# Fewer gate columns before the mixers, modulation steps beside the gate columns, and a tanh in place of a sigmoid, in a two-layer hybrid backbone

## The chip, the cores and the metric

The kernel runs on one core of a Trainium2 chip. The metric is the device time of one execution in microseconds (us). Three runs of the kernel before took 2787.75, 2791.62 and 2795.09 us; their median, 2791.62 us, is the time before.

## The reference, cut to what matters

Two layers work on 512 latent tokens and 256 context tokens of width 1024, in fp32. The second layer gives up the context after its mixers.

```python
mod_l = c_act @ ada_w + ada_b                 # six vectors of 1024: shift, scale and gate, twice
h = modulate(rms_norm(x, norm1_g), sh1, sc1)
daq, dak, dav, lx, ly, gqkv, gz, gb, ga, gate = split_proj(h @ w_in)
da  = differential attention of daq, dak, dav
lru = gelu(ly) * (bidirectional RG-LRU of conv(lx))
gdn = (bidirectional gated DeltaNet of gqkv) * silu(gz)
merged = sum(sigmoid(gate[i]) * ((da, lru, gdn)[i] @ w_branch[i]) for i in range(3))
x = x + g1 * (merged @ w_out)
x = x + g2 * mlp(modulate(rms_norm(x, norm2_g), sh2, sc2))

def rglru_coeffs(xc, gate_w, gate_b, lam):
    r, i = sigmoid(block_diag(xc, gate_w) + gate_b)          # two gates
    log_a = -8.0 * r * softplus(-lam)
    return exp(log_a), sqrt(-expm1(2.0 * log_a)) * (i * xc)

def step(s, xs):                              # DeltaNet, one chunk of tokens, one direction
    v_new = u_n - w_n @ s
    o_n = qd_n @ s + at_n @ v_new
    return s * ge_n + kd_n.T @ v_new, o_n
```

## The kernel before, in words

**Matmuls.** An activation lies in SBUF as 128 channels by up to 768 tokens. Each fp32 product is made of three fp32r products: both factors are split into a high and a low part (`split`, L174 in the profile, a cast on ScalarE and a subtraction on VectorE) and high-high, high-low and low-high are summed in PSUM (`mm_feat`, L201; `mm_tok`, L218). One column block of 128 outputs is 24 pairs of matmuls in the first layer (512 and 256 tokens each) and 24 matmuls of 512 tokens in the second, where context is not needed.

**Weights.** `wunit` loads 512 KB into a tile `raw` of a pool of three (`rp`), splits it into `wh` and `wl` (pools of three), and is done with `raw`.

**Modulation steps.** `ada_steps` is a generator. One round is eight steps and gives a third of the 6144 modulation columns of a layer. A step loads two `raw` tiles of `ada_w` (512 KB each) and adds four 32x512 matmuls into one accumulator `pada` (L344), which is one tile of the PSUM pool `pq` of three (`sm(...)`). The tile is kept from the first step of a round to its eighth, whose result is transposed (`padt`) and added to `L.mod`. The first layer needs round 1 and round 2 of this generator. Round 1 is taken by the projections `gq` and `gv`; round 2 stands in `merge_last`, one step at each of its eight columns. The second layer's own generator is empty; its modulation is computed in the first layer's MLP.

**DeltaNet.** `gdn_inproj` projects q, k and v. `gdn_core` first makes the chunk matrices (transposes L571, products L579 and L582, then a triangular solve of 31 dependent steps on VectorE, L690 and L692, which ends in the transposes L697 and L699). Then comes the recurrence: 24 chunks, both directions side by side. One step is matmuls from the state (L796), copies on ScalarE (L804, L809), the outputs of the step before (L758, L766), matmuls that make the new state (L816, L827 on VectorE), and the start of the next step (L788, L744, L746). Its accumulators `pgd` are `bank`: all three tiles of the pool `pq`, and the one tile of the pool `pf`.

**What is put between.** Behind `gdn_core` in the program stand column blocks that don't need it: `NG[l]` gate columns (`fill_gate`, names `pgt`, `gty`, stored to `gts`), the RG-LRU inputs and gates (`plx`, `py`, `plg`, `lsg`, stored to `lrs`), `gz`, k, v and q. Then come the parts that need the recurrence or the stored columns (`gdn_out`, `lru`, `da_load`, `da_keys`, whose transposes are `pdt`), and the remaining gate columns up to 24. `da_attend` with `merge_first`, `merge_last` (`pml`), the output projection (`pop`) and the MLP (`pm`) follow.

**What sets the order.** The program is traced once, and a scheduler orders the instructions of each engine. It takes what stands first in the program and is ready in its own timing model. A tile of a pool is given out when one is free; an instruction whose tile isn't free yet can't be placed, and others are taken before it. On the chip each engine runs its instructions in the order so fixed.

Of the kernel before, what the change touches and what calls it, by code (L numbers as in the profile page):

```python
# [12 lines left out]
AF = mybir.ActivationFunctionType  # L13
OP = mybir.AluOpType
# [3 lines left out]
T = 768  # L18
# [1 line left out]
TL = 512  # L20
D = 1024
EPS = 1e-6
NG = (12, 16)
NCH = 24
CTXCH = 8
HEADS = 4
# [22 lines left out]
def hybrid_prefix_dit_block_kernel(  # L49
# [8 lines left out]
    V, S, G, PE = nc.vector, nc.scalar, nc.gpsimd, nc.tensor  # L58
# [22 lines left out]
    def big(name):  # L81
        return pb.tile([P, 1024], F32, name=name, tag="b")
# [42 lines left out]
    for q in range(4):  # L125
        r = slice(32 * q, 32 * q + 16)
# [98 lines left out]
    def in_tile(l, col, early=True):  # L225
        return [wunit(w_in[l, :, col:col + P], early)]
# [41 lines left out]
    def load_cols(L, l, rows, mark=None, mark_v=None):  # L268

        r0, r1 = (r[:, :P] for r in rows)  # L270
        ps = big("pcol")
        i = PE.transpose(ps[:, 0:P], r0, ident)
        if mark is not None:
            behind(i, mark)
        PE.transpose(ps[:, P:2 * P], r1, ident)
        L.cols = lp.tile([P, 256], F32, name="cols", tag="cols")
        i = V.tensor_copy(L.cols, ps[:, 0:256])
        if mark_v is not None:
            behind(i, mark_v)
        L.n1 = L.cols[:, 0:8]  # L280
        L.n2 = L.cols[:, 8:16]
        L.adab = L.cols[:, 16:64]
        L.gb = L.cols[:, 80:96]
        L.lam = L.cols[:, 96:104]
        L.gng = L.cols[:, 104:105]
        L.subg = L.cols[:, 105:106]
        L.lcw = L.cols[:, 128:144]
        L.lcb = L.cols[:, 144:148]
        L.gcw = L.cols[:, 148:196]
        V.tensor_scalar(L.gcw, L.gcw, 0.5, None, op0=OP.mult)  # L290
        V.tensor_scalar(L.gng, L.gng, 0.5, None, op0=OP.mult)
        L.mod = lp.tile([P, 48, 2], F32, name="mod", tag=f"mod{l}")
        return L
# [567 lines left out]
        return Z  # L861


    def fill_gate(l, L, a, full, n):
        t0, nt = (0, T) if full else (TC, TL)
        us = in_tile(l, OFF["gate"] + P * n)
        ps = big("pgt")
        mm_feat(ps, us, 0, a, pieces(t0, nt))
        y = t3("gty")
        with tc.high_priority():  # L870
            S.activation(y[:, 0:nt], ps[:, 0:nt], AF.Tanh, scale=0.5)  # L871
        nc.sync.dma_start(gts[n][:, t0:T], y[:, 0:nt])
# [32 lines left out]
    def fill_lx_gates(l, L, j, y, weights):  # L905
        wh, wl = weights
        yh, yl = (gp.tile([P, T], F32R, name="gy", tag="g") for _ in range(2))
        parts = ((0, TC, 512, y[:, 0:TC]), (TC, T, 0, y[:, 259:771]))
        for a0, a1, o, src in parts:
            S.copy(yh[:, a0:a1], src)  # L910
            G.tensor_tensor(yl[:, a0:a1], src, yh[:, a0:a1].bitcast(F32), op=OP.subtract)
        for d in range(2):
            for g in range(2):
                ps = big("plg")
                i = 2 * d + g
                for n, (w, x) in enumerate(((wh, yh), (wh, yl), (wl, yh))):
                    for a0, a1, o, src in parts:
                        PE.matmul(ps[:, o:o + a1 - a0], lhsT=w[:, i, :], rhs=x[:, a0:a1], start=(n == 0), stop=(n == 2))
                r = t3("lsg")
                for a0, a1, o, src in parts:  # L920
                    with tc.high_priority():
                        S.activation(r[:, a0:a1], ps[:, o:o + a1 - a0], AF.Sigmoid,
                                     bias=L.gb[:, 8 * d + 4 * g + j:8 * d + 4 * g + j + 1])
                    if g == 1:
                        G.tensor_tensor(r[:, a0:a1], r[:, a0:a1], src, op=OP.mult)
                nc.sync.dma_start(lrs[j][:, 2 * d + g, :], r[:, 0:T])

    def fill_ly(l, L, a, full, j):
# [57 lines left out]
    def lru_tables(L):  # L986
        L.s8 = lp.tile([P, 8], F32, name="s8", tag="s8")
        L.ns8 = lp.tile([P, 8], F32, name="ns8", tag="ns8")
        nl = tiny("nlam", 8)
        V.tensor_scalar(nl, L.lam, -1.0, None, op0=OP.mult)  # L990
        softplus(L.s8, nl, 8, t3("spl")[:, 0:256])
        V.tensor_scalar(L.ns8, L.s8, 8.0, None, op0=OP.mult)
        V.tensor_scalar(L.s8, L.s8, -8.0, None, op0=OP.mult)

    def lru(l, L, full, mark):
        last = [None]
        t0 = 0 if full else TC
        lh = slab("lh").rearrange("p (k t) -> p k t", k=4)

        def act(*args, **kw):  # L1000
            i = S.activation(*args, **kw)
            if last[0] is not None:
                behind(i, last[0])
            last[0] = i

        for j in range(4):
            W = []
            for d in range(2):
                W.append(slab("lW").rearrange("p (k t) -> p k t", k=4))
                after(nc.sync.dma_start(W[d][:, 0:2, :], lrs[j][:, 2 * d:2 * d + 2, :]), mark)  # L1010
            r, ix, at, u = ([W[d][:, i, :] for d in range(2)] for i in range(4))
            for d in range(2):
                c = slice(4 * d + j, 4 * d + j + 1)
                act(at[d], r[d], AF.Exp, scale=L.s8[:, c])
                act(r[d], r[d], AF.Tanh, scale=L.ns8[:, c])
                act(u[d], at[d], AF.Square)
                V.scalar_tensor_tensor(r[d], u[d], 1.0, r[d], op0=OP.add, op1=OP.mult)
            for d in range(2):
                act(r[d], r[d], AF.Sqrt)
                (V if d else G).tensor_tensor(r[d], r[d], ix[d], op=OP.mult)  # L1020
            yl = ix[1]
            nc.sync.dma_start(yl[:, t0:T], lys[j][:, t0:T])
            hs, a1, b1, u1 = lh[:, j, :], at[1], r[1], u[1]
            V.tensor_tensor_scan(hs, at[0], r[0], 0.0, op0=OP.mult, op1=OP.add)
            V.tensor_tensor_scan(u1[:, TC - 1::-1], a1[:, TC - 1::-1], b1[:, TC - 1::-1], 0.0, op0=OP.mult, op1=OP.add)
            V.tensor_tensor_scan(u1[:, T - 1:TC - 1:-1], a1[:, T - 1:TC - 1:-1], b1[:, T - 1:TC - 1:-1], u1[:, 0:1],
                                 op0=OP.mult, op1=OP.add)
            G.tensor_tensor(hs[:, t0:T], hs[:, t0:T], u1[:, t0:T], op=OP.add)
            V.scalar_tensor_tensor(hs[:, t0:T], yl[:, t0:T], 0.5, hs[:, t0:T], op0=OP.mult, op1=OP.mult)
        return lh  # L1030

    def operands(parts, full):
# [202 lines left out]
                    G.tensor_tensor(gv[0], gv[0], gv[1], op=OP.add)  # L1235
                nc.sync.dma_start(mss[n][:, t0:T], g[0][:, t0:T])

    def merge_last(l, od, full, side):
        t0, nt = (0, T) if full else (TC, TL)
        M = Act("mg", 8)  # L1240
        for b in range(4):
            us = [wunit(w_branch[l, 0, :, 256 * b:256 * b + 256])]
            for n in (2 * b, 2 * b + 1):
                side()
                g, m = gate_of(0, n, t0), t3("ml")
                nc.sync.dma_start(m[:, t0:T], mss[n][:, t0:T])
                ps = big("pml")
                mm_feat(ps, us, P * (n % 2), od, pieces(t0, nt))
                V.scalar_tensor_tensor(g[:, t0:T], g[:, t0:T], 1.0, ps[:, 0:nt], op0=OP.add, op1=OP.mult)
                V.tensor_tensor(m[:, t0:T], m[:, t0:T], g[:, t0:T], op=OP.add)  # L1250
                split(M.hi(n)[:, t0:T], M.lo(n)[:, t0:T], m[:, t0:T])
        return M

# [74 lines left out]
    for i in range(2):  # L1328
        xr.append(slab("xr").rearrange("p (a d) -> p a d", a=3))
        for k in range(3):  # L1330
            t = 3 * i + k
            src = ctx[0, t * P:(t + 1) * P, :] if t < 2 else x[0, (t - 2) * P:(t - 1) * P, :]
# [5 lines left out]
    for half in range(2):  # L1338
        raws.append([])
        for k in range(8):  # L1340
# [3 lines left out]
            src = ada_w[0, k * P:(k + 1) * P, 0:2048].rearrange("p (q c) -> p q c", q=2)  # L1344
# [10 lines left out]
    for t in range(6):  # L1355
        xt = xr[t // 3][:, t % 3, :]
        s = slice(t * P, (t + 1) * P)
        for hf in range(2):
            jk = t3("xsq")
            S.activation(jk[:, 0:512], xt[:, 512 * hf:512 * hf + 512], AF.Square, accum_out=x2[:, 6 * hf + t:6 * hf + t + 1])  # L1360
            ps = sm("pxt")
            for i in range(4):
                n = 4 * hf + i
# [14 lines left out]
    L = Lay()  # L1378
    spill = [(xs[k // 4][:, k % 4, :], x0[k // 4][:, k % 4, :]) for k in range(8)]
    for l in range(DEPTH):  # L1380
        full = l < DEPTH - 1
        a = norm(xT, L, L.n1, 0, 8, "hn", halves(True)) if l else norm0(xT, L, raws, {0: mark_pe, 2: marks[-1]}, lambda i: load_cols(L, 0, vrows, i, mark_v))
        dump(f"hn{l}", a.h[0].bitcast(F32))
        steps = ada_steps(l, L, (1, 2) if l == 0 else ())
# [5 lines left out]
        gdn_core(l, L, R, full)  # L1390
        dump(f"go{l}", R.o)
        for n in range(NG[l]):
            fill_gate(l, L, a, full, n)
        Q = da_tables(l)
        lru_tables(L)
        y = fill_lx(l, L, a, full, 0)
# [30 lines left out]
        od = da_finish(L, Q, full)  # L1427
        dump(f"odh{l}", od.h[0].bitcast(F32))
        if stop == "da":
            return  # L1430
        M = merge_last(l, od, full, lambda: next(steps, None))
        xT = out_proj(l, L, M, full)
        dump(f"xa{l}_0", xT[0])
        dump(f"xa{l}_1", xT[1])
# [2 lines left out]
        a = norm(xT, L, L.n2, 24, 32, "hm", halves(full))  # L1437
# [5 lines left out]
        steps = ada_steps(l + 1, L2, (0, 1, 2)) if full else iter(())  # L1443
# [7 lines left out]
        if full:  # L1451
            L = L2
            spill = [(xs[k // 4][:, k % 4, :], xT[k // 4][:, k % 4, :]) for k in range(8)]

    for t in range(2, 6):
        for hf in range(2):
            ps = sm("pfo")
            for i in range(4):
                PE.transpose(ps[:, i * P:(i + 1) * P], xT[hf][:, i, t * P:(t + 1) * P], ident)
            o = t3("fo")  # L1460
# [28 lines left out]
```

## Time and profile before

| | before |
|---|---|
| time, median of three runs | 2791.62 us |
| time of the profiled execution | 2792.77 us |
| span of its trace | 2791.1 us |
| PE busy | 2651.8 us (95%) |
| DVE busy | 1487.5 us (53%) |
| ACT busy | 1104.9 us (40%) |
| POOL busy | 553.6 us (20%) |

PE is TensorE's matmuls, PEld its weight loads, DVE is VectorE, ACT is ScalarE, POOL is GpSimd. Times in the trace count from the start of the span. A busy PE is not a PE at its peak: matmuls are pipelined and their spans overlap. PEclk is the granted TensorE clock as a share of full speed.

### The profile page before, as it was taken

To read this page: it belongs to the slowest core of one execution; us is meant where nothing else is said; L and a number is where in the kernel's file an instruction comes from. 1 tells how busy PE (TensorE), PEld (TensorE's weight loads), DVE (VectorE), ACT (ScalarE), POOL (GpSimd) and SP (SyncE) were. 2 spreads that over 40 slices of the span, in tenths; PEclk is the share of its full clock that TensorE was granted. 3 is DMA by queue.
4 is the path that set the end of the run, shared out by engine and by line. 5 is a ranking of instruction groups with operands and counts; after the bars stand their busy time and mean duration, and the time that the engine had idled before them with its cause. 6 is when DMAs were issued, how large, how long until landed. Compare 5 with 4: busy or idle time off the path is not lost. (4 is left out here: it accounts for less than half of the span.)

```text
span 2791.1 us, 44891 instructions
## 1 busy us (share of the span) xinstructions
PE 2651.8 (95%) x17973; PEld 2256.7 (81%) x17973; DVE 1487.5 (53%) x2477; ACT 1104.9 (40%) x2058; POOL 553.6 (20%) x693
## 2 busy tenths in 40 slices
PE   7999999997999899999999999999998798899999
PEld 4778888996888688888888888777997687788887
DVE  5659554567375443333333476775437776544444
ACT  4343454465465233221122253445436755432321
POOL 3001343223112022110101130034322311221110
PEclk8999999998999999999999999999999699999999
DMA  7432233254423723333332222334224443333332
GB/s 261 127 111 89 84 104 101 77 168 142 145 99 106 250 81 110 125 106 114 121 114 76 89 78 76 107 104 144 84 68 145 166 125 103 98 106 92 97 99 76
DMA packets 315592, 318.71 MB, mean 114 GB/s; under 512 B 19500, under 2 KB 268408, under 8 KB 314488
## 3 DMA queue, kind: packets, MB, share of 16 engines
q1 hardware_dynamic: 315384, 315.84, 36.0%
q8 instruction: 142, 2.33, 0.4%
q14 instruction: 66, 0.54, 0.1%
HBM read 259.70 MB, written 56.10 MB: 113 GB/s over the span
## 5 line engine op out<-in xcount | busy, mean ns | idle before, releaser
L174 ACT CAST wh<-raw 128x1024 fp32r<-128x1024 f32 x288 | 302.6, 1051 | 969.0 <-PE pm L201 624.3
L174 DVE TENSOR_TENSOR wl<-raw,wh 128x1024 fp32r<-128x1024 f32 x288 | 368.0, 1278 | 453.6 <-ACT wh L174 441.2
L201 PE MATMUL pm<-hdh,wh 128*128 128x256 f32 (+1 forms) x896 | 297.4, 332 | 0.5
L201 PE MATMUL pm<-hdl,wh 128*128 128x256 f32 (+1 forms) x896 | 294.5, 329 | 0.0
L201 PE MATMUL pm<-hdh,wl 128*128 128x256 f32 (+1 forms) x896 | 294.3, 328 | 0.0
L1315 DVE SCALAR_TENSOR_TENSOR xT<-pm,mod,xT 128x256 f32<-128x256 f32 (+1 forms) x224 | 133.8, 598 | 237.5 <-PE pm L201 237.5
L201 PE MATMUL pm<-hmh,wh 128*128 128x512 f32 (+1 forms) x800 | 242.5, 353 | 4.4 <-ACT mr L1297 2.8
L201 PE MATMUL pm<-hml,wh 128*128 128x512 f32 (+1 forms) x800 | 243.6, 354 | 3.1 <-DVE hml L457 3.1
L1299 POOL TENSOR_TENSOR mq<-mr 128x768 f32<-128x768 f32 (+1 forms) x64 | 107.2, 1675 | 692.4 <-ACT mr L1297 684.7
L201 PE MATMUL pm<-hmh,wl 128*128 128x512 f32 (+1 forms) x800 | 240.7, 350 | 0.0
L201 PEld LDWEIGHTS pm<-hdh,wh 128*128 128x128 f32 x896 | 170.1, 190 | 30.2 <-DVE xT L1315 7.5
L201 PE MATMUL pgt<-hnh,wh 128*128 128x512 f32 x576 | 181.1, 365 | 8.8 <-ACT gty L871 8.8
L201 PEld LDWEIGHTS pm<-hdh,wl 128*128 128x128 f32 x896 | 170.0, 190 | 15.2
L201 PEld LDWEIGHTS pm<-hdl,wh 128*128 128x128 f32 x896 | 170.2, 190 | 14.8
L201 PE MATMUL pgt<-hnl,wh 128*128 128x512 f32 x576 | 178.8, 364 | 0.0
L201 PE MATMUL pgt<-hnh,wl 128*128 128x512 f32 x576 | 178.4, 363 | 0.0
L201 PEld LDWEIGHTS pm<-hmh,wh 128*128 128x128 f32 x800 | 134.9, 191 | 32.2 <-ACT wh L174 5.9
L201 PEld LDWEIGHTS pm<-hml,wh 128*128 128x128 f32 x800 | 135.5, 191 | 23.4 <-DVE hml L457 4.1
L201 PEld LDWEIGHTS pm<-hmh,wl 128*128 128x128 f32 x800 | 136.4, 191 | 21.5
L201 PEld LDWEIGHTS pgt<-hnh,wh 128*128 128x128 f32 x576 | 98.5, 193 | 26.9 <-ACT gty L871 10.3
L201 PE MATMUL pg<-hnh,wh 128*128 128x256 f32 (+1 forms) x368 | 103.9, 348 | 8.9 <-ACT hnh L407 4.7
L201 PEld LDWEIGHTS pgt<-hnh,wl 128*128 128x128 f32 x576 | 97.7, 193 | 16.3
(428 smaller groups left out, 6103.1 us busy)
## 6 DMA issues: line engine op xcount, KB each, us to landing
raw<-in_mlp_w_dram SPq DMA_DIRECT2D x128, 512.0 KB, 3.8
raw<-in_w_in_dram SPq DMA_DIRECT2D x120, 512.0 KB, 4.0
raw<-in_ada_w_dram SPq DMA_DIRECT2D x80, 512.0 KB, 3.9
lrs<-lsg SPq DMA_DIRECT2D x32, 384.0 KB, 2.4
lW<-lrs SPq DMA_DIRECT2D x16, 768.0 KB
raw<-in_w_branch_dram SPq DMA_DIRECT2D x24, 512.0 KB, 5.4
gts<-gty SPq DMA_DIRECT2D x24, 384.0 KB, 4.8
mgg<-gts SPq DMA_DIRECT2D x24, 384.0 KB, 3.5
```

The costliest lines, as they stand in the source:

```text
L174: return S.copy(hi, src), V.tensor_tensor(lo, src, hi.bitcast(F32), op=OP.subtract)
L201: last = PE.matmul(ps[:, o:o + n], lhsT=w, rhs=r[:, t0:t0 + n], start=(k == 0 and i == 0), stop=(k == nk - 1 and i == 2))
L1299: G.tensor_tensor(q[:, 0:nt], r[:, 0:nt], r[:, 0:nt], op=OP.mult)
L1315: V.scalar_tensor_tensor(xv, ps[:, 0:m], L.mod[:, 40 + n, v:v + 1], xv, op0=OP.mult, op1=OP.add)
```

## The change

There are four edits.

1. `NG` goes from (12, 16) to (10, 12): that many gate columns stand before the RG-LRU inputs; the other 14 and 12 stand behind the mixers.
2. The step of round 2 is taken out of `merge_last` and put into `fill_gate`, behind the weight unit of the column. The first eight gate columns of the first layer take the eight steps.
3. The RG-LRU gates are `tanh(0.5 x)` in place of `sigmoid(x)`; the factors 0.5 and the added 1 move into the bias, the decay factors (8 becomes 4, with a bias) and the last factor (0.5 becomes 0.25).
4. The product of the input gate with its input, 32 instructions in all, goes from GpSimd to VectorE, which adds 1 in the same instruction.

```diff
-NG = (12, 16)
+NG = (10, 12)
...
+        V.tensor_scalar(L.gb, L.gb, 0.5, None, op0=OP.mult)
...
-    def fill_gate(l, L, a, full, n):
+    def fill_gate(l, L, a, full, n, side=None):
         t0, nt = (0, T) if full else (TC, TL)
         us = in_tile(l, OFF["gate"] + P * n)
+        if side:
+            side()
         ps = big("pgt")
...
-                        S.activation(r[:, a0:a1], ps[:, o:o + a1 - a0], AF.Sigmoid,
+                        S.activation(r[:, a0:a1], ps[:, o:o + a1 - a0], AF.Tanh, scale=0.5,
                                      bias=L.gb[:, 8 * d + 4 * g + j:8 * d + 4 * g + j + 1])
                     if g == 1:
-                        G.tensor_tensor(r[:, a0:a1], r[:, a0:a1], src, op=OP.mult)
+                        V.scalar_tensor_tensor(r[:, a0:a1], r[:, a0:a1], 1.0, src, op0=OP.add, op1=OP.mult)
...
-        V.tensor_scalar(L.ns8, L.s8, 8.0, None, op0=OP.mult)
-        V.tensor_scalar(L.s8, L.s8, -8.0, None, op0=OP.mult)
+        V.tensor_scalar(L.ns8, L.s8, 4.0, None, op0=OP.mult)
+        V.tensor_scalar(L.s8, L.s8, -4.0, None, op0=OP.mult)
...
-                act(at[d], r[d], AF.Exp, scale=L.s8[:, c])
-                act(r[d], r[d], AF.Tanh, scale=L.ns8[:, c])
+                act(at[d], r[d], AF.Exp, scale=L.s8[:, c], bias=L.s8[:, c])
+                act(r[d], r[d], AF.Tanh, scale=L.ns8[:, c], bias=L.ns8[:, c])
...
-            V.scalar_tensor_tensor(hs[:, t0:T], yl[:, t0:T], 0.5, hs[:, t0:T], op0=OP.mult, op1=OP.mult)
+            V.scalar_tensor_tensor(hs[:, t0:T], yl[:, t0:T], 0.25, hs[:, t0:T], op0=OP.mult, op1=OP.mult)
...
-    def merge_last(l, od, full, side):
+    def merge_last(l, od, full):
...
-                side()
                 g, m = gate_of(0, n, t0), t3("ml")
...
-            fill_gate(l, L, a, full, n)
+            fill_gate(l, L, a, full, n, lambda: next(steps, None))
...
-        M = merge_last(l, od, full, lambda: next(steps, None))
+        M = merge_last(l, od, full)
```

The order that comes of it is shown at three places. In the change line numbers are 1 to 3 higher.

PE, first layer, from the last product of the chunk matrices on (`psq`); `pgt` is a gate column. Before:

```order
L597 MATMUL psq<-ones,gq_1810 32x1 x16
L201 MATMUL pgt<-hnh,wh 128x512
L201 MATMUL pgt<-hnh,wh 128x256
L201 MATMUL pgt<-hnl,wh 128x512
L201 MATMUL pgt<-hnl,wh 128x256
L201 MATMUL pgt<-hnh,wl 128x512
L201 MATMUL pgt<-hnh,wl 128x256
```

The same place in the change:

```order
L598 MATMUL psq<-ones,gq_1811 32x1 x16
L660 MATMUL pge<-ident,eg 128x128 x2
L789 MATMUL pgd<-gW 128x128 x2
L817 MATMUL pgd<-gW,gA 128x128 x3
L817 MATMUL pgd_2005<-gW,gA 128x128
L817 MATMUL pgd<-gW,gB 128x128 x3
L817 MATMUL pgd_2005<-gW,gB 128x128
L745 MATMUL pgd<-gW 128x128 x2
```

In the order before, 366 matmuls of gate columns stand between `psq` and the first matmul of the recurrence (`pgd`); in the change there are only the two of `pge`.

PE, first layer, within one step of the recurrence. Before:

```order
L796 MATMUL pgd<-gB,gW 32x128 x4
L796 MATMUL pgd<-gB,gQT 32x128 x4
L796 MATMUL pgd<-gA,gW 32x128 x4
L796 MATMUL pgd<-gA,gQT 32x128 x4
L758 MATMUL pgd_2004<-gW 128x128 x2
L201 MATMUL pgt<-hnh,wl 128x512
L201 MATMUL pgt<-hnh,wl 128x256
L201 MATMUL pgt<-hnh,wh 128x512
```

The last step of the recurrence in the change, and what follows it (`pada` is the accumulator of round 2):

```order
L797 MATMUL pgd<-gA,gQT 32x128 x4
L759 MATMUL pgd_2005<-gW 128x128 x2
L345 MATMUL pada<-raw,cact 32x512 x4
L759 MATMUL pgd_2005<-gW 128x128 x2
L345 MATMUL pada<-raw,cact 32x512 x4
L201 MATMUL pgt<-hnh,wh 128x512
L201 MATMUL pgt<-hnh,wh 128x256
```

Before, from `psq` to the last L758, 576 pairs of matmuls of 512 and 256 columns (gate columns, `plx`, `py`, `plg`, `pz`) and 635 matmuls of 256 columns (`pqk`, `pv`) stand among the matmuls of the recurrence. In the change none does in the first layer: the first `pada` is placed when the recurrence is over, and the gate columns from the third on behind it; no engine has a piece of them between its instructions of the recurrence.

SP, which issues the loads, first layer, around the second gate column. Before:

```order
L872 DMA gts_138<-gty 128x768
L166 DMA raw<-in_w_in_dram 128x8x128
L872 DMA gts_139<-gty 128x768
L166 DMA raw<-in_w_in_dram 128x8x128
L872 DMA gts_140<-gty 128x768
```

The same place in the change:

```order
L342 DMA raw<-in_ada_w_dram 128x1024
L166 DMA raw<-in_w_in_dram 128x8x128
L342 DMA raw<-in_ada_w_dram 128x1024 x2
L166 DMA raw<-in_w_in_dram 128x8x128
L342 DMA raw<-in_ada_w_dram 128x1024 x2
```

The loads of `ada_w` stand between those of the gate columns, in the same pool of three. In the second layer the recurrence stays interleaved with column blocks. Before, its last five groups of L796 stand without other matmuls between them, in the change its last seven; four gate columns of 24 matmuls have moved behind it.

## Rows read from the trace of the kernel before

**Rows 1.** The page's line of busy times.

```profile
PE 2651.8 (95%) x17973; PEld 2256.7 (81%) x17973; DVE 1487.5 (53%) x2477; ACT 1104.9 (40%) x2058; POOL 553.6 (20%) x693
```

**Rows 2.** Busy time by stretch; columns stand in the first row.

```profile
core 0: us, PE busy (x) PEld busy (x) DVE busy (x) ACT busy (x) POOL busy (x), PEclk, DMA share, GB/s
205.00:588.00 383.00, 378.03 (x3213) 328.06 (x3208) 218.65 (x486) 158.51 (x382) 112.08 (x190) 0.99 0.29 93
588.00:770.00 182.00, 163.63 (x1025) 147.50 (x1023) 113.13 (x149) 104.73 (x143) 51.00 (x26) 0.93 0.49 159
896.00:958.00 62.00, 53.24 (x293) 37.98 (x293) 30.31 (x40) 13.66 (x18) 4.27 (x5) 0.94 0.65 214
2127.00:2230.00 103.00, 82.02 (x363) 68.44 (x362) 82.63 (x106) 83.03 (x107) 37.13 (x22) 0.79 0.60 209
```

**Rows 3.** Busy time by stretch of the recurrence's accumulators alone: PE, PEld, DVE, ACT.

```profile
272.00:585.00 313.00, 100.33 (x1384) 78.77 (x1384) 61.69 (x230) 32.95 (x140) 1.00 0.30 95
```

**Rows 4.** Timeline of PE in a gate column: start, duration, line, operation.

```profile
212.30 0.52 PE L201 MATMUL pgt<-hnh,wh 128*128 128x512 f32 x2
213.37 0.51 PE L201 MATMUL pgt<-hnh,wh 128*128 128x512 f32 x2
```

**Rows 5.** Timeline of PE in a block of q.

```profile
2069.75 0.28 PE L218 MATMUL pqk<-wh,hnh 128*128 128x256 f32 x1
2070.47 0.28 PE L218 MATMUL pqk<-wh,hnh 128*128 128x256 f32 x1
```

**Rows 6.** Busy time of VectorE and ScalarE in line L174 during the solve.

```profile
205.00:272.00 67.00, 7.33 (x6) 7.37 (x7) 0.96 0.28 90
```

**Rows 7.** Timeline of PE, second layer, last five groups of L796.

```profile
2095.18 0.42 PE L796 MATMUL pgd<-gB,gW 128*32 128x128 f32 x8
...
2100.74 0.66 PE L796 MATMUL pgd<-gB,gW 128*32 128x128 f32 x8 [0.65 <-ACT gW L746]
...
2108.69 0.65 PE L796 MATMUL pgd<-gB,gW 128*32 128x128 f32 x8 [1.60 <-ACT gW L746]
...
2116.39 0.66 PE L796 MATMUL pgd<-gB,gW 128*32 128x128 f32 x8 [0.52 <-ACT gW L746]
...
2122.47 0.43 PE L796 MATMUL pgd<-gB,gW 128*32 128x128 f32 x8 [0.52 <-ACT gW L746]
```

**Rows 8.** Busy time by stretch, columns as in rows 2: bare steps, round 1.

```profile
76.00:160.00 84.00, 84.00 (x519) 62.98 (x518) 50.33 (x63) 24.08 (x36) 2.47 (x28) 1.00 0.45 133
...
2095.20:2122.50 27.30, 23.02 (x245) 18.07 (x245) 14.72 (x54) 10.41 (x36) 6.80 (x16) 0.75 0.00 1
```

**Rows 9.** Waits of PE, 585 to 770: us in total, times, longest.

```profile
PE pdt L1099 <- DVE dkx L174: 9.2, 1, 9.2
PE pgt L201 <- ACT gty L871: 5.5, 2, 5.3
```

**Rows 10.** Waits of PE, 885 to 1010.

```profile
PE pada L344 <- DMA raw<-in_ada_w_dram: 4.1, 4, 1.9
PE pml L201 <- ACT wh L174: 2.4, 2, 1.4
```

**Rows 11.** Waits of PE, 2127 to 2230.

```profile
PE pdt L1099 <- DVE dkx L174: 10.6, 9, 3.5
PE pdt L1099 <- ACT dkx L174: 5.7, 1, 5.7
```

**Rows 12.** The instructions of the RG-LRU gates on ScalarE and GpSimd: duration ns min/median/max.

```profile
L922 ACT ACTIVATE lsg<-plg,cols x64: 467/596/725, 337.7 to 1937.0; 128x256 f32<-128x256 f32 x32, 128x512 f32<-128x512 f32 x32
L922 ACT ACT_TABLE_LOAD  x2: 1283/1283/1283, 336.4 to 1860.6; - x2
L925 POOL TENSOR_TENSOR lsg<-lsg,ly x32: 722/1285/2127, 340.0 to 1938.5; 128x256 f32<-128x256 f32 x16, 128x512 f32<-128x512 f32 x16
```

**Rows 13.** A product with an added 1 on VectorE, the same view.

```profile
L1249 DVE SCALAR_TENSOR_TENSOR mgg<-mgg,pml x8: 678/689/690, 2352.8 to 2376.0; 128x512 f32<-128x512 f32 x8
```

## The prediction

> **What bounds the kernel now.** I read the page's busy times first: PE is busy for 95% of the span, no other engine for more than 53% [rows 1]. So the time is PE's work plus what PE loses, and an edit counts where it changes one of these. The busy times by stretch come next [rows 2]. In the first layer's solve and recurrence, 205 to 588 us, PE is busy for 378 of 383 us at a clock of 0.99, although the recurrence's own matmuls are only 100 us of it [rows 3]: the rest are column blocks put between its steps. This stretch loses almost nothing because it has such work. Behind it, 588 to 770, PE loses 18 us at a clock of 0.93; around the last merge, 896 to 958, 9 us; in the second layer behind the recurrence, 2127 to 2230, 21 us at a clock of 0.79 [rows 2]. Those three places have something to gain.
>
> **The order decides the main term.** The accumulator of round 2 is a tile of the pool of three that the recurrence holds in full, so the first step placed in a gate column gets its tile only when the recurrence is over. Until then the step's raw tiles are kept, two for each step, out of a pool of three, so the third gate column gets no weights either, nor does any block behind it. The order of the change shows just that: no column block stands in the first layer between the chunk products and the end of the recurrence. PE takes its instructions in order, so this doesn't depend on how long anything takes on the chip.
>
> **First layer, solve.** It is VectorE's chain. Before, it ran from 205 to 272, with six splits for gate columns in it, 7.3 us [rows 6]. Without them: 67 - 7 = 60 us, with PE idle.
>
> **First layer, recurrence.** What a step takes when nothing stands between is shown by the second layer's end, where the blocks had run out: five groups of L796 start at 2095.18, 2100.74, 2108.69, 2116.39 and 2122.47 [rows 7], so steps of 5.56, 7.95, 7.70 and 6.08 us, 6.82 us in the mean. The clock of that stretch is 0.75 [rows 8], and the rows show both levels: eight matmuls take 0.42 us at 2095 and 0.65 us from 2100 to 2116, at 2.4 and 1.2 GHz. 24 steps at the mean are 164 us; at the shortest, 133; at the longest, 191. I take 164, since the same chain of the same tiles alternates between the two levels there. Restarting the column blocks costs PE a split on each of two engines behind the recurrence; the longest comparable wait is 5.3 us [rows 9]. I take 5, ends 0 and 10.
>
> The Trainium skill, TensorE: Matmul & The Clock Gate, part 1, HAM oscillation, says that pauses between bursts of matmuls bring the array back to half its clock, burst after burst. That speaks against this change, and the trace agrees in part: the clock falls in the bare steps but comes back before they end. By the rule alone every step would be a half-clock one, which is the rival at 2906 below.
>
> **First layer, what comes back.** The blocks that stood there are done later. 576 pairs of matmuls: three pairs take 213.37 - 212.30 = 1.07 us [rows 4], 0.357 us each, 206 us. 635 matmuls of 256 columns: six take 2070.47 - 2069.75 = 0.72 us [rows 5], 0.12 us each, 76 us. Together 282 us; from the other side, 383 - 5 idle - 100 own [rows 2, 3] = 278. I take 280. Sum for the first layer: 60 + 164 + 5 + 280 - 383 = +126 us.
>
> **First layer, behind the recurrence.** 18 us of idle time [rows 2] are mostly one wait of the keys' transposes for VectorE, 9.2 us, and waits for a gate column's evacuation, 5.5 us [rows 9]. With 280 us more of matmuls in front, the mixers' chains on VectorE and ScalarE have far more to hide behind, and most of this should go. Against it, the blocks' own short chains (convolution, products, splits) now stand without the recurrence between them. I take -10, ends -18 and +10.
>
> **Last merge of the first layer.** 96 pairs at 0.357 us are 34 us; with transposes and start some 40, against 62 now [rows 2]: -22. The stretch moves 214 GB/s, and PE waits in it for the step's loads and for splits [rows 10]; both have this cause. The eight steps' matmuls come back in the gate columns. Round 1 shows what they cost there: 84 us without idle time for 519 matmuls [rows 8], 64 of them the steps', and 455 / 2 x 0.357 = 81 us for the others; so +3 us. The sum is -19; I take -15, because the merge keeps its loads of gates and sums, ends -8 (the idle time alone) and -20.
>
> **Second layer.** Four columns of 24 matmuls of 512 leave the recurrence: 0.357 - 0.12 = 0.237 us each, 22.8 us. Two more intervals go bare: 2 x (6.82 - 100/24) = +5.3 us [rows 3, 7]. So the recurrence ends 17.5 us earlier. Behind it 22.8 us of matmuls are added to a stretch with 21 us idle, where the keys wait 16 us for their splits [rows 2, 11], but VectorE and ScalarE are at 80% and each column brings them a split. I take +8.5 there, so -9 in all, ends -17 and +5.
>
> **Gates by tanh.** The sigmoid cost two table loads of 1.28 us in all [rows 12], and ScalarE is busy for 40%: 0, ends -2.6 and +5. 32 products leave GpSimd at 1.29 us each; on VectorE one of 512 columns takes 0.69 us [rows 12, 13], so at most 32 x 0.69 = 22 us on an engine at 53%, hidden behind PE: 0, ends 0 and +5. The halved bias and the added bias operands: 0.
>
> **Sum.** The profiled execution took 2792.8 us, 1.7 us more than its span; the median of the runs is 1.2 us lower. 2792.8 + 126 - 10 - 15 - 9 = 2885 us, 3.3% slower.
>
> **Rivals.**
> - *The recurrence keeps the full clock* and runs at 5.56 us a step: 24 x 5.56 = 133, so 2854 us. For it: the first and last bare steps [rows 7]. Against it: the solve before it leaves PE idle for 60 us.
> - *It stays at half clock* at 7.70 us a step: 185, so 2906 us. For it: that idle time, and two steps in rows 7. Against it: the return to 0.43 us a group at 2122.
> - *The loads stall the columns behind the recurrence.* Eight columns with a step move 1.5 MB in some 9 us, 170 GB/s, between the 133 of round 1, which never waited [rows 8], and the 214 of the merge, which did [rows 2, 10]. Eight waits of 1.9 us are 15, and the merge's gain is lost again; with the evacuations' 5 us twice, 2910 us.
> - *Not slower.* The three gains alone would give 2793 - 34 = 2759 us. This needs the bare recurrence to cost no more than its blocks give back: 60 + 24 b + 5 + 280 - 383 - 34 = 0 at b = 3.0 us a step. The state's matmuls alone are 100 / 24 = 4.2 us a step [rows 3], so the point isn't in reach unless blocks run inside the recurrence after all, which the order excludes.
>
> **How the numbers follow.** Forecast 0.50, full clock 0.20, half clock 0.18, stalled loads 0.10, not slower 0.02. Beyond 0.3%, some 8 us, a difference can be told from none: faster 0.01, same 0.01, slower 0.98. The range holds the first four cases with the smaller terms' ends in part: from 2854 less half of the lows' 22 us, about 2840, to 2910 and about half of the highs' 40, 2930.
>
> **What would show it.** In the changed profile: a stretch of about 230 us in the first layer with PE's share well under 0.8 in the recurrence and near zero in the solve, a clock between 0.5 and 1, and chains of L797, L759, L817, L789, L745 that nothing interrupts, 5.6 to 7.7 us apart. Behind it a stretch from the third gate column to the keys with almost no idle time, no wait of 9 us for the keys, and a last merge of some 40 us. In the second layer seven bare groups, and a shorter stretch behind. The prediction is wrong if column blocks stand in the first layer's recurrence, if a bare step is under 5 us there, or if the columns with steps wait for `raw`.

## The result: 3% slower, and the profile after

The changed kernel takes 2873.77 us (median of 4 runs, 2870.9 to 2882.06) against 2789.68 us of the kernel before, run beside it (2786.11 to 2795.09): a ratio of 1.0305, 95% interval 1.0287 to 1.0323. The forecast was 2885 us. The profiled execution took 2870.9 us, its span is 2869.2 us.

From the page of the changed kernel: the busy times, and of its forty slices PE's busy tenths, PE's clock and the bytes moved.

```profile
PE 2666.3 (93%) x17973; PEld 2271.3 (79%) x17973; DVE 1495.5 (52%) x2511; ACT 1105.7 (39%) x2054; POOL 485.0 (17%) x661
...
PE   7973889998999998999999999999998898999999
...
PEclk9986979999999999999999999999999889999999
...
GB/s 261 127 75 1 2 66 179 138 176 199 107 136 105 108 157 56 125 118 115 114 117 118 59 103 61 75 132 142 86 67 129 187 114 98 134 89 96 96 98 78
```

Against [rows 1] PE does the same 17973 matmuls, and its share falls from 95% to 93%. In the slices one place stands out: in the fourth and fifth (215 to 359 us) the core moves 1 and 2 GB/s, so it loads next to nothing there. Busy time by stretch of the changed kernel, columns as in [rows 2]:

```profile
203.10:259.00 55.90, 1.43 (x17) 1.05 (x10) 53.76 (x102) 6.28 (x14) 5.87 (x6) 0.50 0.02 7
259.00:404.60 145.60, 120.15 (x1395) 92.31 (x1396) 74.23 (x261) 65.80 (x232) 58.70 (x141) 0.87 0.01 2
404.60:418.00 13.40, 9.27 (x35) 6.34 (x34) 8.21 (x20) 4.18 (x6) 0.00 (x0) 0.62 0.67 197
418.00:856.00 438.00, 427.56 (x2742) 381.95 (x2741) 184.90 (x250) 180.49 (x251) 55.75 (x52) 0.99 0.49 156
...
1010.00:1047.00 37.00, 34.93 (x202) 29.96 (x201) 25.99 (x29) 11.22 (x13) 2.53 (x3) 1.00 0.67 207
1855.00:1941.00 86.00, 82.03 (x370) 67.84 (x368) 83.91 (x154) 32.71 (x58) 15.12 (x27) 0.93 0.37 111
1941.00:2192.00 251.00, 240.09 (x2269) 207.30 (x2268) 129.44 (x327) 112.85 (x307) 68.55 (x133) 1.00 0.28 84
2192.00:2310.00 118.00, 102.77 (x463) 84.68 (x462) 89.81 (x111) 89.43 (x115) 37.27 (x22) 0.88 0.62 208
```

The first two rows answer to the first of [rows 2]. In the solve PE is busy for 1.4 of 56 us, in the recurrence it has 1395 matmuls, the 1384 of the recurrence alone [rows 3] and few more. The third is the restart, the fourth the work that came back, the fifth the last merge, 37 us where the window of [rows 2] is 62 (56 by the marks of the table below). The last three are solve, recurrence and what lies behind it in the second layer.

Why nothing is put between: SP's timeline of the changed kernel, over 210 us (start, duration, queue, line, operation).

```profile
202.04 1.44 SPq L622 DMA_DIRECT2D alc<-in_gdn_A_log_dram  x2
404.28 0.35 SPq L342 DMA_DIRECT2D raw<-in_ada_w_dram  x1
404.72 0.39 SPq L166 DMA_DIRECT2D raw<-in_w_in_dram  x1
```

Between 203.5 and 404.3 us SP issues no load: the raw tiles are held by steps whose accumulator comes only with the recurrence's end. PE's timeline around that end, in brackets the wait before an instruction and who ended it:

```profile
402.96 1.28 PE L345 MATMUL pada<-raw,cact 128*32 128x512 f32 x8
404.17 0.71 PE L759 MATMUL pgd<-gW 128*128 128x128 f32 x4
408.30 1.94 PE L345 MATMUL pada<-raw,cact 128*32 128x512 f32 x8 [3.41 <-DMA raw<-in_ada_w_dram]
410.95 1.01 PE L201 MATMUL pgt<-hnh,wh 128*128 128x512 f32 x2 [0.72 <-ACT wh L174]
```

The first `pada` stands before the recurrence's last matmul, the second waits for a load, and the gate column starts at half clock (1.01 us for two matmuls, 0.52 in [rows 4]). What a step takes when nothing stands between shows in groups of L797 (an interval from one to the next is a step):

```profile
290.83 0.66 PE L797 MATMUL pgd<-gB,gW 128*32 128x128 f32 x8 [0.65 <-ACT gW L747]
297.82 0.65 PE L797 MATMUL pgd<-gB,gW 128*32 128x128 f32 x8 [0.65 <-ACT gW L747]
304.72 0.43 PE L797 MATMUL pgd<-gB,gW 128*32 128x128 f32 x8 [0.65 <-ACT gW L747]
...
310.26 0.43 PE L797 MATMUL pgd<-gB,gW 128*32 128x128 f32 x8 [0.65 <-ACT gW L747]
...
385.26 0.65 PE L797 MATMUL pgd<-gB,gW 128*32 128x128 f32 x8 [2.72 <-DVE oss L844]
392.97 0.66 PE L797 MATMUL pgd<-gB,gW 128*32 128x128 f32 x8 [0.52 <-ACT gW L747]
```

Busy time by stretch of three such steps, columns as in [rows 2]:

```profile
310.26:315.71 5.45, 4.61 (x60) 3.58 (x60) 2.64 (x10) 2.80 (x11) 2.77 (x8) 1.00 0.01 3
290.83:297.82 6.99, 5.98 (x61) 4.61 (x61) 3.13 (x12) 2.90 (x11) 2.50 (x7) 0.74 0.01 2
385.26:392.97 7.71, 7.05 (x60) 5.75 (x61) 3.80 (x13) 2.17 (x9) 0.88 (x2) 0.50 0.00 0
```

A step takes 5.45 us at 2.4 GHz (granted clock 1.00), 7.0 where it begins at 1.2 GHz and the clock comes back within it (0.74), 7.7 where it stays at 1.2 GHz to its end (0.50), and once 9.0 where an output's VectorE work came late (385.26 follows 376.25). Of the 23 groups with a state 16 show 0.43 us and 7 show 0.63 to 0.66.

Stages by PE's own marks in the profiled runs (us): the end of the first layer's chunk products to the first `pgd` (solve), to the last (recurrence), to the first scores, and so on. The stages left out move by 2.4 us or less.

| stage | before | after | change |
|---|---|---|---|
| start to end of chunk products | 205.3 | 203.1 | -2.2 |
| layer 1: solve | 67.4 | 55.9 | -11.5 |
| layer 1: recurrence | 315.2 | 145.6 | -169.6 |
| layer 1: to the scores | 173.0 | 463.6 | +290.6 |
| layer 1: last merge | 56.1 | 37.0 | -19.1 |
| layer 1: output projection | 78.3 | 75.7 | -2.6 |
| layer 2: solve | 73.8 | 86.2 | +12.4 |
| layer 2: recurrence | 286.3 | 250.6 | -35.7 |
| layer 2: to the scores | 103.6 | 118.7 | +15.1 |
| start to last matmul | 2786.1 | 2864.2 | +78.1 |

### The profile page after: what moved, and what is told of

Read it like the earlier page. It is cut to its first block, busy times and chain, and to the rows that moved or that the text cites. A ratio compares the mean times of both kernels' runs of the same rounds, so it can differ in the third digit from the quotient of the medians.

```text
span 2869.2 us, 45003 instructions
## 1 busy us (share of the span) xinstructions
PE 2666.3 (93%) x17973; PEld 2271.3 (79%) x17973; DVE 1495.5 (52%) x2511; ACT 1105.7 (39%) x2054; POOL 485.0 (17%) x661
## 4 chain that ended last, share of the span: by engine, by line
PE 81%; ACT 6%; DVE 6%; issue 3%; DMA 2%; POOL 0%; SPq 0%; DVEq 0%; ACTq 0%; POOLq 0%
PE pm L201 31%; PE pgt L201 10%; PE pg L201 7%; PE pop L201 4%; PE pqk L218 4%; PE pmf L201 3%; PE plx L201 2%; PE py L201 2%; PE pz L201 2%; PE pv L218 2%; PE pgd L797 2%; ACT lW L1004 1%; PE pada L345 1%; PE pml L201 1%; PE pgd L817 1%
## 5 line engine op out<-in xcount | busy, mean ns | idle before, releaser
L174 ACT CAST wh<-raw 128x1024 fp32r<-128x1024 f32 x288 | 302.2, 1049 | 1002.9 <-PE pm L201 626.5
L174 DVE TENSOR_TENSOR wl<-raw,wh 128x1024 fp32r<-128x1024 f32 x288 | 367.0, 1274 | 533.7 <-ACT wh L174 520.5
L201 PEld LDWEIGHTS pm<-hdh,wl 128*128 128x128 f32 x896 | 170.3, 190 | 15.1
L201 PE MATMUL pg<-hnh,wh 128*128 128x256 f32 (+1 forms) x368 | 103.6, 348 | 8.5 <-ACT hnh L408 4.6
```

The source lines that it names most:

```text
L174: return S.copy(hi, src), V.tensor_tensor(lo, src, hi.bitcast(F32), op=OP.subtract)
L201: last = PE.matmul(ps[:, o:o + n], lhsT=w, rhs=r[:, t0:t0 + n], start=(k == 0 and i == 0), stop=(k == nk - 1 and i == 2))
```

## The experiments

Theory: the loss is edit 2 alone, and in it the accumulator `pada` in the pool that the recurrence holds. The rivals put the loss on the steps' loads and place among the gate columns, on the fewer gate columns (edit 1), or on the gates (edits 3 and 4). Ratios are to the kernel before, run on the same chip.

**Edits 1, 3 and 4 without edit 2.** The changed kernel with the steps back in `merge_last`.

```diff
-            fill_gate(l, L, a, full, n, lambda: next(steps, None))
+            fill_gate(l, L, a, full, n)
...
-        M = merge_last(l, od, full)
+        M = merge_last(l, od, full, lambda: next(steps, None))
```

> The change with round 2 of the modulation put back into the last merge; fewer gate columns in front, tanh and the product on VectorE stay. Theory (the accumulator of the round is a tile that the recurrence holds, so steps in the front gate columns shut every column block out of the first layer's recurrence): the blocks return into the recurrence, the stretch of 200 us without a load goes, and the time is about 2780 us (2765 to 2795), the 10 us under before coming from the second layer. Rival (the lower numbers of gate columns, or the gates by tanh with their product on VectorE, are what costs): it stays at 2860 us or more.

2795.09 us, ratio 1.0015 (1.0001 to 1.0029). The loss is gone: solve 66.5, recurrence 315.2, to the scores 171.6 us, as before. The expected gain of 10 us isn't there either: the time is just above the expected range, and by the run of edit 1 alone below, edits 3 and 4 cost a little more than edit 1 gains.

**Edit 2 alone.** The kernel before with the steps in its first gate columns.

```diff
         for n in range(NG[l]):
-            fill_gate(l, L, a, full, n)
+            fill_gate(l, L, a, full, n, lambda: next(steps, None))
...
-        M = merge_last(l, od, full, lambda: next(steps, None))
+        M = merge_last(l, od, full)
```

> The kernel before with the move of the steps alone: 12 and 16 gate columns in front, sigmoid, product on GpSimd. Theory: the whole loss is here, and without the second layer's gain of 10 us it is some 90 us: about 2880 us (2865 to 2895). Rival (the numbers of gate columns are what costs): about 2775 us, the gain of the merge alone.

2882.85 us, 1.0328 (1.0299 to 1.0358): the whole loss. Its solve and recurrence, busy times by stretch:

```profile
203.00:258.00 55.00, 1.23 (x4) 0.93 (x4) 52.86 (x99) 6.28 (x14) 5.52 (x5) 0.50 0.01 3
258.00:401.00 143.00, 117.09 (x1396) 90.07 (x1396) 74.58 (x263) 65.92 (x233) 58.81 (x142) 0.90 0.01 2
```

They are those of the changed kernel: 1396 matmuls in the recurrence, none of a column.

**The same steps, another PSUM pool.** In the changed kernel only the accumulator is moved, out of the pool that the recurrence holds.

```diff
-            ps = sm("pada")
+            ps = big("pada")[:, 0:512] if (l, r) == (0, 2) else sm("pada")
```

> The change with one edit: the accumulator of round 2 in the first layer is half of a tile of the pool of two that the column blocks use, not a tile of the pool of three that the recurrence takes in full. The steps stay in the front gate columns and their loads in the pool of three raw tiles. Theory (the accumulator's tile is the cause, the raw tiles are only what it holds): the steps end before the recurrence begins, the blocks return into it, about 2770 us (2755 to 2795), with some waits for the one accumulator tile that is left to the gate columns. Rival (the raw tiles that the steps take are the cause by themselves): about 2865 us.

2798.47 us, 1.0027 (1.0016 to 1.0038). With the loads, the steps and their places as in the change the 3% are gone, so the accumulator's pool is the cause, and the rival (the raw tiles by themselves) is out. The first row is the recurrence, the second from there to the scores:

```profile
268.00:590.00 322.00, 311.93 (x2770) 269.60 (x2769) 160.71 (x394) 137.09 (x351) 87.20 (x166) 0.99 0.28 89
590.00:787.50 197.50, 183.02 (x1140) 164.77 (x1139) 110.55 (x137) 104.20 (x132) 41.53 (x25) 0.95 0.50 159
```

The columns stand in the recurrence again, PE busy for 312 of 322 us. The expected 2770 us was a miss, above its range: the stretch behind takes 197.5 us, not 173, and it isn't idle time (14.5 us); PE has 183 us of work there. The steps take room in front of the recurrence, gate columns move from there into it, and blocks of q and k move out behind it: 288 matmuls of `pqk` stand there, 96 in the kernel of the first experiment; the 192 more, at 0.12 us each [rows 5], are an estimated 23 us. That is more than the merge's 20 us, and layer 2's three stages, 465 us against 464 before, show no gain here.

**The steps behind the recurrence, accumulator unchanged.**

```diff
         for n in range(NG[l]):
-            fill_gate(l, L, a, full, n, lambda: next(steps, None))
+            fill_gate(l, L, a, full, n)
...
         for n in range(NG[l], 24):
-            fill_gate(l, L, a, full, n)
+            fill_gate(l, L, a, full, n, lambda: next(steps, None))
```

> The change with the eight steps moved to the first eight gate columns behind the mixers, so they are not placed before the recurrence is over. Theory: as with the steps in the merge, and the last merge keeps its gain of some 19 us less some 3 us for the steps in the columns: about 2765 us (2750 to 2780). Rival (1.5 MB for each column stall the columns wherever they stand): eight waits of 2 us, no gain over the steps in the merge, about 2785 us or more.

2816.34 us, 1.0101 (1.0077 to 1.0126), against the expected 2765: a miss, with the same mechanism. Behind the recurrence the pool `pq` serves the keys' transposes `pdt`. Busy times by stretch:

```profile
590.00:620.00 30.00, 26.85 (x169) 23.88 (x168) 24.38 (x48) 26.59 (x31) 6.33 (x5) 0.94 0.59 198
620.00:650.00 30.00, 3.66 (x19) 3.02 (x18) 28.23 (x26) 22.69 (x25) 16.94 (x9) 0.60 0.50 178
650.00:680.00 30.00, 23.29 (x95) 20.52 (x98) 17.91 (x21) 15.05 (x27) 7.84 (x5) 0.50 0.03 8
```

From 620 to 650 PE is busy for 3.7 us, and then works at half clock while the core moves 8 GB/s. SP's timeline and PE's waits of this kernel:

```profile
601.40 0.34 SPq L342 DMA_DIRECT2D raw<-in_ada_w_dram  x1
...
681.61 0.33 SPq L342 DMA_DIRECT2D raw<-in_ada_w_dram  x1
681.99 0.43 SPq L166 DMA_DIRECT2D raw<-in_w_in_dram  x1
```

```profile
PE pdt L1102 <- ACT dkx L174: 24.8, 4, 24.0
```

The first matmul of the steps stands behind the last of the keys' transposes (679.3 us):

```profile
679.65 1.94 PE L345 MATMUL pada<-raw,cact 128*32 128x512 f32 x8
```

Between 601 and 682 us SP issues no weights of a gate column, so nothing stands before the keys' wait: 24.0 us in one piece, where before it was 9.2 [rows 9].

**A free accumulator and late steps.** `pada` of round 2 takes the one tile of the pool `pf`, which is idle behind the recurrence, and the steps stand in the last eight gate columns. Tried on the changed kernel and on the kernel before; the second is edit 2 made so, alone.

```diff
-            ps = sm("pada")
+            ps = pf.tile([P, 512], F32, name="pada", tag="f") if (l, r) == (0, 2) else sm("pada")
...
         for n in range(NG[l], 24):
-            fill_gate(l, L, a, full, n)
+            fill_gate(l, L, a, full, n, (lambda: next(steps, None)) if n >= 16 else None)
```

> The change with the accumulator of round 2 in the pool pf, whose one tile is free between the recurrence and the first merge, and the eight steps at the last eight gate columns behind the mixers. Theory (steps cost only where they hold a tile that the work beside them needs, and their loads fit under gate columns): the recurrence, the keys and the columns keep their order, and the last merge keeps its gain of 19 us less 3: about 2778 us (2768 to 2790). Rival (1.5 MB for each column stall the columns, or the gain in the merge reappears as waits elsewhere): 2790 us or more.

> The kernel before with this move of the steps alone (accumulator in pf, last eight gate columns), 12 and 16 columns in front, sigmoid, product on GpSimd. Theory: 2791 - 16 = about 2775 us (2765 to 2785). Rival as for the run before: 2788 us or more.

On the changed kernel 2777.52 us, 0.9960 (0.9947 to 0.9973); on the kernel before 2774.46 us, 0.9949 (0.9936 to 0.9963). Both times are as expected: with this move the kernel before is 0.5% faster. No run has the free accumulator without the late place or the other way round, so the two aren't told apart. It isn't all gain. The stretch behind the recurrence, in the kernel before with this move:

```profile
585.00:773.00 188.00, 170.07 (x1036) 142.84 (x1035) 105.87 (x135) 100.16 (x127) 48.64 (x25) 0.93 0.59 195
```

It grows from 173 to 188 us, while the merge falls from 56 to 37 and the projection from 78 to 75: 22 us won, 15 given back by the profile. So the expected 16 us, 19 of the merge less 3 for the steps, were met in part by luck: these stages give 7, the whole first layer 10. The second layer's recurrence is 6 us shorter in the profile, though PE has the same matmuls in the same order there. Half of that lies in its bare steps, which took 27.3 us at a clock of 0.75 before [rows 8] and with the move take 24.3 at 0.93:

```profile
2082.00:2106.30 24.30, 19.90 (x241) 15.20 (x240) 14.84 (x54) 10.12 (x36) 6.75 (x16) 0.93 0.00 1
```

Why the clock differs there isn't shown, so a few of the 14 us aren't traced to the move.

**Fewer gate columns alone (edit 1).** In the kernel before:

```diff
-NG = (12, 16)
+NG = (10, 12)
```

> The kernel before with 10 and 12 gate columns in front and nothing else changed. Open is what the change's other edits do in the second layer, where the solve took 86 us against 74 and the recurrence 251 against 286. Theory (with fewer gate columns in front, the RG-LRU inputs fall into the solve, and their convolutions hold up its chain on VectorE; it is the numbers of columns that do it): second-layer solve about 85 us, recurrence about 255, stretch behind it about 118, sum 5 to 10 us under before; time 2780 to 2792 us. Rival (the products moved to VectorE hold the solve up): the solve stays at 75 to 78 us and the time is 2775 us or less.

2779.02 us, 0.9963 (0.9948 to 0.9978), 1 us under the expected range. Solve 83.4, recurrence 257.6, behind 116.3 us in the second layer: near the stages of the changed kernel there (86.2, 250.6, 118.7) and 6 us under before in sum, so these are edit 1's.

**The gates: edits 3 and 4, then each alone.** In the kernel before, both, as in the diff of the change; the product on VectorE with the sigmoid kept; the tanh with the product left on GpSimd, as a plain product (it leaves out the added 1).

```diff
-                        S.activation(r[:, a0:a1], ps[:, o:o + a1 - a0], AF.Sigmoid,
+                        S.activation(r[:, a0:a1], ps[:, o:o + a1 - a0], AF.Tanh, scale=0.5,
...
-                        G.tensor_tensor(r[:, a0:a1], r[:, a0:a1], src, op=OP.mult)
+                        V.scalar_tensor_tensor(r[:, a0:a1], r[:, a0:a1], 1.0, src, op0=OP.add, op1=OP.mult)
```

> The kernel before with the gates by tanh and the product on VectorE alone; steps in the merge, 12 and 16 columns in front. Theory (PE sets the time, the two table loads and the 32 products are off its path): the same as before within 0.2%, 2786 to 2797 us. Rival (VectorE's extra 20 us, all in front of or inside the recurrences, delay their steps): 2800 us or more.

> The kernel before with the sigmoid kept and only the 32 products of the RG-LRU input gate moved from GpSimd to VectorE. Open is which half of the pair (gates by tanh, product on VectorE) made that pair 0.55% slower. Theory A (the engine move does it: VectorE works on the recurrences' steps and on the blocks' splits in the same queue): 2800 us or more. Theory B (the tanh does it, by another order of table loads and blocks): 2786 to 2793 us, no difference.

```diff
-                        G.tensor_tensor(r[:, a0:a1], r[:, a0:a1], src, op=OP.mult)
+                        V.tensor_tensor(r[:, a0:a1], r[:, a0:a1], src, op=OP.mult)
```

> The kernel before with edit 3 alone: gates by tanh, the products left on GpSimd as plain products. The added 1 in the product is left out, so what the kernel computes differs in that one place, while every instruction is of the kind and size of before. What is told apart: the whole of edits 3 and 4 cost 0.55%, edit 4 alone (with the sigmoid kept) 0.23%. Theory A, each edit has its own price: the tanh alone costs the difference, 0.3%, so 2795 to 2803 us beside a before of 2790. Theory B, the tanh alone saves its two table loads and costs nothing of its own, and the 0.55% is the product on VectorE, whose order turns out a little differently beside the tanh: 2786 to 2793 us.

| kernel | us | ratio | layer 1 recurrence | table loads at the `act` of `lru` |
|---|---|---|---|---|
| both | 2805.36 | 1.0055 (1.0041 to 1.0069) | 322.3 | 22 |
| product on VectorE | 2797.71 | 1.0023 (1.0013 to 1.0032) | 322.3 | 22 |
| tanh | 2794.00 | 1.0012 (1.0001 to 1.0024) | 315.2 | 15 |

Before, the recurrence is 315.2 us and there are 19 such loads. The groups of table loads on ScalarE with both edits (busy us, mean ns):

```profile
L1004 ACT ACT_TABLE_LOAD x22 | 28.2, 1283 | 0.4
L134 ACT ACT_TABLE_LOAD x11 | 14.1, 1283 | 2.1 <-DVE dso L1193 1.9
```

The two loads of the sigmoid [rows 12] are gone, but three more have come at L1004 and one at L134. Edit 4 costs 7 us in the first layer's recurrence, with the tanh and without, and the tanh alone none there. That price belongs to the order with 12 columns in front: with 10, the recurrence takes 313.1 us (edit 1 alone) and 315.2 with edits 3 and 4 added (the first experiment). The two prices, 0.23% and 0.12%, make 0.35% where both together cost 0.55%; theory A had the tanh at 0.3%, theory B at nothing, and neither holds. By the profiles the rest has a place: behind the second layer's recurrence both together take 110.3 us, either alone 104, and before it was 103.6. Its cause stays open.

**Both gains together.** The kernel before with edit 1 and the late steps in `pf`, without edits 3 and 4.

> The two parts that gained, together: the kernel before with 10 and 12 gate columns in front, and the steps at the last eight columns behind the mixers with their accumulator in pf; sigmoid and the product on GpSimd as before. If the two gains add (9.5 and 14 us, in different layers): 2765 us (2758 to 2772), under both kernels and under the same with tanh and VectorE (2777.5 us). If the gate columns' gain needs the other order of loads: about 2775 us.

2772.97 us, 0.9941 (0.9928 to 0.9955), slower than the 2765 expected and near the 2775 of the other case: 0.37% and 0.51% don't add up in full. By the profile the merge and projection give 23 us and the second layer's three stages 10, the stretch behind the first recurrence takes 11 back. This is the lowest ratio of all kernels tried, below both of the case; its interval overlaps that of the move alone, so those two aren't told apart.

```profile
PE 2643.6 (96%) x17973; PEld 2248.2 (81%) x17973; DVE 1480.5 (53%) x2477; ACT 1106.2 (40%) x2059; POOL 539.7 (19%) x693
```

PE's share is 96%; 8 us of its busy time are gone against [rows 1].

## Why the prediction was right, and where its sizes were off

The mechanism was the one forecast, and it was shown by the change of the accumulator's pool alone. The loss was forecast as 92 us; the medians differ by 84, the profiled runs by 78. The terms, against the profile:

- *Solve, 60 us.* It took 55.9, PE idle in nearly all of it: right.
- *Recurrence, 164 us, ends 133 and 191.* It took 145.6. This is the largest mis-sized term. It went by the mean of four intervals [rows 7], of which one stood at 1.2 GHz throughout (granted clock 0.50), two in part (0.71 and 0.88) and one not at all. Here 16 of 23 groups are at 2.4 GHz, and the stretch has a clock of 0.87 against their 0.75 [rows 8]. The rival at full clock, 133, was nearer than the one at half clock, 185.
- *Restart 5, blocks back 280, behind the recurrence -10, the steps +3.* From 173 that makes 451 us; measured 463.6. The keys' wait of 9.2 us [rows 9] is gone, as said. What PE waits for most from 404 to 856 us in the changed kernel:

```profile
PE pada L345 <- DMA raw<-in_ada_w_dram: 3.4, 1, 3.4
PE pv L218 <- DVE wl L174: 2.5, 2, 1.7
PE pv L218 <- ACT wh L174: 1.6, 1, 1.6
```

  Small waits for weights and their splits have taken its place: over the whole stretch PE idles for 17.1 us (463.4 less 446.3 busy), before for 17.5 (173 less 155.5). So the -10 didn't come, the restart included. PE's work there grew by 290.8 us, not 283: the blocks' 280 are about right, and the steps' 3 are too few. The steps' matmuls alone, in this stretch and in round 1 of the kernel before, from which the 3 was worked out (PE busy, PEclk, DMA share, GB/s):

```profile
404.60:868.00 463.40, 8.33 (x56) 0.97 0.50 158
76.00:160.00 84.00, 9.54 (x64) 1.00 0.45 133
```

  So the difference of 84 and 81 us hid a cost of 9.5. In the kernel before with the late steps the same stretch, otherwise with the same matmuls, is 15 us longer. The rival with stalled loads had the place right (`raw` is waited for) and not the size: one wait of 3.4 us, not eight.
- *Last merge, -18 in the stage (the -15 without the steps' +3).* -19.1, and -2.6 in the projection behind it: right.
- *Second layer, -9.* The three stages give 12.4 - 35.7 + 15.1 = -8.2 us: the sum is right, its parts were not, so that is luck. The recurrence's end comes 23 us earlier (17.5 forecast), the stretch behind it is 15 us longer (8.5 forecast in the sum, though the signs speak of "a shorter stretch behind"). The solve, forecast unchanged, takes up work: two groups of VectorE's lines in it, its own chain and convolutions, six at 1 us, about half of its 12 us (before, no convolution stands in that solve):

```profile
L693 DVE TENSOR_TENSOR gA<-gA,gC 128x62 f32<-128x62 f32 (+15 forms) x31 | 17.1, 552 | 0.6
...
L480 DVE SCALAR_TENSOR_TENSOR ly<-lx,cols,ly 128x771 f32<-128x771 f32 x6 | 6.1, 1018 | 0.0
```

- *Gates by tanh and the product on VectorE, 0, ends -2.6 and +10.* In the kernel before the two cost 0.55%, some 15 us, beyond the upper end; on top of edit 1 they cost 0.52 points (first experiment against edit 1 alone), on top of edit 1 and the late steps 0.19. "The sigmoid cost two table loads" failed: the number of loads is set by the order of ScalarE, not by the function alone. "Hidden behind PE" failed for the product by 7 us of a recurrence in the kernel before. How much of it is in the changed kernel is open: its first recurrence has no gate blocks, so those 7 us can't be there.

Solve and recurrence came 22 us under the forecast, the stretch behind 13 over; with the merge 4 under, that is most of the 14 us between 92 and 78. The two misses point opposite ways, so the total was closer than its terms by luck.

Of the signs, most came: no column block in the recurrence, a clock of 0.87, no long wait of the keys, seven bare groups in the second layer. Four didn't. PE's share in the recurrence is 0.83 (120.15 of 145.60 us), not well under 0.8; the steps are 5.45 to 9.0 us apart, not 5.6 to 7.7; the stretch behind the second layer's recurrence isn't shorter; and a column with a step did wait for `raw`, once, 3.4 us at the restart, which the prediction had named as a sign of being wrong.

The Trainium skill, TensorE: Matmul & The Clock Gate, part 1, HAM oscillation, tells of a loop in which each burst of matmuls waits for a load for longer than the burst lasts, so that every burst begins at half clock. The trace agrees behind the solve, where the first group ran at 1.2 GHz. The bare steps, with waits of 0.65 us, aren't that case, so the page doesn't make every step a half-clock one, as the prediction took it: 16 of 23 groups were at 2.4 GHz. Why six later ones were not is open.

## What to carry to other kernels

Before a step is moved, ask from which pool its accumulator comes and who holds that pool at the new place: a tile kept over several steps shuts in with it every load tile that these steps hold, and so every block that shares them, here 200 us without one load. A wait that is moved out of one stage should go where its tiles are free and the loads have room; with the steps moved so the kernel was 0.5% faster, where they had cost 3.3%. Work that moves takes its own time along: of the 22 us won in the merge and the projection, 15 came back among the columns. And an elementwise product moved to a half-idle engine can cost time (0.23% here), so it is worth a run by itself.

## What was not expected of the chip

- A chain of short matmul groups with a wait of 0.65 us ahead of each step held 2.4 GHz for 13 steps in a row (304.72 to 370.71, groups of 0.43 us), and the group at 376.25 us ran at 1.2 GHz, after steps like the ones before: no wait of PE in them was longer than 0.65 us.
- After 56 us of an almost idle PE the first group ran at half clock (0.66 us at 267.98) and the next, 6 us later, at full (0.43 at 273.99).
- A bare step with the clock at its full level takes 5.45 us (PE busy for 4.61); one wholly at half clock takes 7.71 (PE busy for 7.05), 2.3 us more and not a doubling.
